# RWKV's two halves with buffers of their own, GDN behind them, gates as fp32 products

## The chip, the cores and the metric

The kernel runs on one core of a Trainium2 chip: five compute engines with a queue each (PE for matrix products, DVE for vector work, ACT for activations and copies, POOL for general vector work, SP, which here issues transfers) and 16 DMA engines, around an on-chip buffer (SBUF) and a small accumulator memory that PE writes (PSUM). The metric is the device time of one execution in microseconds, as the median of several runs. Each engine takes its instructions in the order in which the program has them and waits at each until its inputs and buffers are ready.

## The reference

The program is two networks, one behind the other, for 256 tokens of width 1024. The first (two feed-forward layers and four attention branches) isn't touched. The second is a mixing sublayer and a mixture of experts; the mixing sublayer takes the normed and modulated u and does this:

```python
a_lat, b_lat, gates_lat = jnp.split(u_lat @ w_in, split_at, axis=-1)
oa_lat, _ = run_a(a_lat, state_a)                      # gated DeltaNet (GDN)
ob_lat, _ = run_b(to_col_major(b_lat, rows), state_b)  # RWKV-7
y = jax.nn.sigmoid(g_a) * (o_a @ w_o_a) + jax.nn.sigmoid(g_b) * (o_b @ w_o_b)
return y @ w_out
```

Both branches are linear recurrences over the tokens, run in both directions. The step of RWKV is S = S(diag(w) + a bᵀ) + v kᵀ, y = S r; that of GDN is S = a(I - b k kᵀ)S + b k vᵀ, o = Sᵀ q. The states at the start come from a context sequence, which is done much earlier in the program. The output must be right to single precision.

## The kernel before

The recurrences are computed in chunks: for every chunk the products among its tokens form a triangular matrix, the inverse of which is found once for all chunks, and then a short chain carries the state from chunk to chunk. RWKV works on chunks of 64 tokens, four steps for each direction, and its eight heads go in two halves of four (`rwkv_half`, hf 0 and 1). A half has four parts:

- the *factors*: `first` makes decays, keys and their products from the projected columns (DVE lines 1520 to 1553: kdr, th, the scan cum, gam, AR, BK), `second` masks the products of tokens with tokens (Mak, Ur, Mr, lines 1569 to 1574), and copies bring the values into SV (line 1485);
- the *inverse* (`inverse`, lines 951 to 1046): a transposed copy Ut of the matrix, fifteen columns on DVE (pairs of Pb and Yb, lines 975 and 977), two transposes Yc, then small products on PE (ps_inv) with copies by DVE, ACT and POOL in between, to the last copy Ur. GDN's matrix is of 128 and takes one level more (D, Q, U, lines 1032 to 1045);
- the *gate* (`rwkv_gate`: pgate, yg, yz);
- the *chain* of four steps: rhs (line 1632), the product psa, its copy to SV (1638), the new state Sr (1657).

GDN (`gdn`, lines 1157 to 1345) has a setup (G, tv, row products rowp), normalised keys and queries, factors and products (Eb, E, U, qk), the same inverse, and a state chain (pks, r, Sa, oa).

In `mix` the projections come first: pieces of w_in are loaded, each is split into a rounded half wh (on ACT) and a rest wl (on DVE), and a product is three products of such halves (`mm3`, lines 102 to 104). Then RWKV is written with a high priority, then GDN and the gates. `gates_ahead` computes the 2048 gate columns: for 64 pieces of weights of 128x256 a load, the split wh on ACT (line 2229), wl on POOL (line 2230), and two `mm3`; it reads u back from DRAM, where the norm stored it in its two halves. Nothing before the merge needs its result, and the scheduler spreads its products over the stage. `merge` multiplies oa and ob with their output weights, applies the gates and makes the split of the merged product for the last projection; the experts follow, whose 96 MB of weights are streamed.

A scheduler decides the order of each engine's queue when the program is built, from the dependences, the buffers, priorities and its own estimate of durations. Buffers of a pool are handed out by tag; a tile of the same tag waits until the older one is no longer read. Both halves' sets (AR, BKT, U, R1, SV, Mr) had the same tags in one pool, so the second half's had to wait until the first half was through with them. In PSUM, RWKV had the tags g and s with two buffers each, and GDN with the gates had a (three buffers) and w (one).

Of the kernel before, what the change touches and what calls it, by code (L numbers as in the profile page):

```python
# [31 lines left out]
class Core:  # L32
# [142 lines left out]
    def norm_pair(self, pool, x, rs, A, B=None, keep=None, save=None):  # L175
# [7 lines left out]
        for t in range(2):  # L183
# [17 lines left out]
            if save is not None:  # L201
                for i, v in enumerate((hh, hl)):
                    nc.sync.dma_start(out=save[:, i, :, ts], in_=v[:, :, ts].bitcast(F32))
# [719 lines left out]
class Block2:  # L923
# [135 lines left out]
    def proj(self, u, w, start, n, evict):  # L1059
# [5 lines left out]
        for f0 in range(0, n, 256):  # L1065
            pg = k.ps("g", [P, 2, T], "pg")
            for g0 in range(f0, min(f0 + 256, n), wide):
                m = min(wide, n - g0)
                wr = k.raw(w[:, start + g0: start + g0 + m].rearrange("(c p) f -> p c f", p=P), [P, KC, m])
                for h0 in range(0, m, P):  # L1070
                    mm = min(P, m - h0)
                    fi = (g0 + h0 - f0) // P
                    for c0 in range(0, KC, cs):
# [286 lines left out]
class Rwkv(Block2):  # L1360
# [69 lines left out]
    def rwkv_proj(self, u, w, colmajor):  # L1430

        return tuple(self.rwkv_part(name, u, w, colmajor) for name in "vkwr")

    def rwkv(self, cols, S0, with_out, name, Sout=None, ob=None):


# [7 lines left out]

# [19 lines left out]
        out = None  # L1464
        for hf in range(2):

            SV = pool.tile([P, 2, 4, 4, 64], F32, tag="SV", name="SV")
            for d in range(2):
                vh = vT[:, 2 * hf:2 * hf + 2]
                if d == 1:  # L1470
                    vr = pool.tile([P, 2, T], F32, tag="t2", name="vTb", bufs=self.t2)
                    nc.vector.tensor_copy(vr, rev(vh))
                    vh = vr
                for t in range(2):
                    pt = k.ps("s", [P, 2, P], "ptv")
                    for p in range(2):
                        nc.tensor.transpose(pt[:, p], vh[:, p, t * P:(t + 1) * P], k.ident)
                    for q in range(2):
                        for h in range(2):
                            i = pt[64 * q:64 * q + 64, :, 64 * h:64 * h + 64]  # L1480
                            o = SV[64:128, h, 2 * t + q, 2 * d:2 * d + 2]
                            if h == 0:
                                nc.scalar.activation(o, i, AF.Copy)
                            else:
                                nc.vector.tensor_copy(o, i)
            out = self.rwkv_half(hf, kT, rT, lo, kk, SV, None if S0 is None else S0[:, hf],
                           with_out, name + str(hf), None if Sout is None else Sout[:, hf], vT, ob, out)
        if with_out:
            out()

    def rwkv_half(self, hf, kT, rT, lo, kk, SV, S0, with_out, name, Sout, vT, ob, before):
# [6 lines left out]
        R1 = pool.tile([P, 4, 4, 64], F32, tag="R1", name="R1")  # L1498
        gam = pool.tile([P, 4, 4], F32, tag="gam", name="gam")
        Mr = None  # L1500
        if with_out:
            Mr = pool.tile([P, 4, 2, 4, 64], F32, tag="Mr", name="Mr")
            bon = pool.tile([P, 2, 4], F32, tag="bon", name="bon")
# [101 lines left out]
        if before is not None:  # L1605
            before()
        XT = self.inverse(U, 16, 64)
        if with_out:
            gate = self.rwkv_gate(hf, bon, vT, lo[:, 2])
        if with_out:  # L1610
            yp = [k.ps("g", [P, 2, 2, 64], "yr") for _ in range(2)]

        def outputs(c, lhs, rhs, first, last):

            for d in range(2):
                cn = 3 - c if d else c
                for pl in range(2):
                    for h in range(2):
                        nc.tensor.matmul(yp[h][64 * (cn % 2):64 * (cn % 2) + 64, cn // 2, pl], lhs(h, 2 * d + pl),
                                         rhs(h, 2 * d + pl), start=first and pl == 0, stop=last and pl == 1)  # L1620

        hb = (slice(0, 64), slice(64, P))
        S = S0
        for c in range(4):
            rhs = R1[:, c]
            if S is not None:
                pa = k.ps("s", [P, 4, 64], "pa")
                for pd in range(4):
                    for b in (slice(0, 64), slice(64, P)):
                        nc.tensor.matmul(pa[b, pd], AR[b, pd, c, 0], S[b, pd], start=True, stop=True)  # L1630
                rhs = pool.tile([P, 4, 64], F32, tag="rhs", name="rhs")
                nc.vector.tensor_tensor(rhs, pa, R1[:, c], op=OP.add)
            px = [k.ps("s" if with_out else "g", [P, 4, 64], "psa") for _ in range(2)]
            for pd in range(4):
                for h, b in enumerate(hb):
                    nc.tensor.matmul(px[h][0:64, pd], XT[b, 4 * pd + c], rhs[b, pd], start=True, stop=True)
            nc.scalar.activation(SV[0:64, 0, c], px[0][0:64], AF.Copy)
            nc.vector.tensor_copy(SV[0:64, 1, c], px[1][0:64])
            if with_out:
                outputs(c, lambda h, pd: AR[hb[h], pd, c, 1], lambda h, pd: S[hb[h], pd], c == 0, False)  # L1640
            if c == 3 and with_out:
                outputs(c, lambda h, pd: Mr[:, pd, h, c], lambda h, pd: SV[:, h, c, pd], False, True)
                break
            pS = k.ps("s", [P, 4, 64], "pSr")
            for pd in range(4):
                for h in range(2):
                    b = slice(64 * h, 64 * h + 64)
                    nc.tensor.matmul(pS[b, pd], BKT[:, pd, c, b], SV[:, h, c, pd], start=True, stop=True)
            if c == 3:
                Sn = Sout  # L1650
            else:
                Sn = pool.tile([P, 4, 64], F32, tag="Sr", name="Sr", bufs=3)
            gb = gam[:, c].unsqueeze(2).to_broadcast([P, 4, 64])
            if S is None:
                nc.vector.tensor_tensor(Sn, pS, gb, op=OP.mult)
            else:
                nc.vector.tensor_tensor(Sn, pS, S, op=OP.add)
                (nc.vector if with_out else nc.gpsimd).tensor_tensor(Sn, Sn, gb, op=OP.mult)
            if with_out:
                outputs(c, lambda h, pd: Mr[:, pd, h, c], lambda h, pd: SV[:, h, c, pd], False, False)  # L1660
            S = Sn
        if not with_out:
            return
        y = self.keep.tile([P, 2, 256], F32, tag="yrw", name="yrw")
        for h in range(2):
            nc.scalar.activation(y.rearrange("p t (a h b) -> p h t a b", h=2, b=64)[:, h], yp[h], AF.Copy)
        return lambda: self.rwkv_out(hf, y, gate, ob)


class Tail(Rwkv):  # L1670
# [439 lines left out]
    def ctx_second(self):  # L2110

        k = self.k
        with k.use(g=k.banks["s"]):
# [3 lines left out]
            with k.pool("rcl", "right") as self.keep, k.pool("rc", "right") as self.pool:  # L2117
                self.t2 = 6
                self.rwkv(self.ctx_load("vkw") + [None], None, False, "rc", Sout=self.Sb)
# [27 lines left out]
    def begin(self, x, pool):  # L2147
# [4 lines left out]
        self.u_lat = self.dram.tile([P, 2, KC, T], F32, name="u_lat")  # L2152
        half = lambda v, q: v[:, q * 512:q * 512 + 512]
        with k.pool("lx", "right") as xp:
# [24 lines left out]
            with k.use(s=k.banks["a"]):  # L2179
                return k.norm_pair(xp, x, both, am, bm, pool, self.u_lat)  # L2180

    def mix(self, start):
# [4 lines left out]
        with ExitStack() as right, ExitStack() as left:  # L2187
            gk = self.gk = right.enter_context(k.pool("gk", "right"))
            gf = right.enter_context(k.pool("gf", "right"))
            proj = ExitStack()  # L2190
            up = proj.enter_context(k.pool("up", "right"))
            wp = Weights(proj.enter_context(k.pool("uw", "right")), 2048, 2, 1024, 3)
# [238 lines left out]
```

## Time and profile before

| | |
|---|---|
| median of 3 runs | 2396.19 us (2391.33 to 2402.87) |
| the profiled execution | 2390.7 us, of which the span 2389.0 |
| PE busy | 2249.9 us (94% of the span), mean granted clock 0.953 |
| DVE busy | 1689.7 us (71%) |
| ACT busy | 1199.8 us (50%) |
| POOL busy | 344.1 us (14%) |
| DMA | 450.91 MB, mean 189 GB/s |

The shares are means over stages that differ. The stage in question is short, from about 1633 to 2041 us of the span. The view by stage gives the busy time of each engine in a stretch and the clock that PE was granted; the view in order of time gives the start and length of each instruction, the number of equal ones merged into a row after the x, and, in brackets, how long the engine stood idle before it and what ended that.

### The profile page before, as it was taken

What the parts mean: (1) busy time and instruction counts of PE and PEld (TensorE: products, weight loads), DVE (VectorE), ACT (ScalarE), POOL (GpSimd) and SP (SyncE); (2) the same over time, 40 slices, a digit from 0 to 9 for tenths busy, and PEclk for the clock granted to TensorE, in tenths of its full rate; (3) what the DMA queues carried; (4) which work ended last, traced back from release to release, by engine and by line L of the source; (5) the groups of instructions that cost most, each with busy time, mean ns of one, the idle gap of its engine ahead of it and who ended that gap; (6) DMA issues with size and microseconds to landing.
All of it is one profiled execution on the core that took longest, in us unless ns stands there. A gap on an engine that the chain in (4) does not pass through costs nothing. (4 is left out here: it accounts for less than half of the span.)

```text
span 2389.0 us, 46279 instructions
## 1 busy us (share of the span) xinstructions
PE 2249.9 (94%) x19065; PEld 2041.7 (85%) x19065; DVE 1689.7 (71%) x2796; ACT 1199.8 (50%) x1919; POOL 344.1 (14%) x465
## 2 busy tenths in 40 slices
PE   7999999999999999999999999998989887899997
PEld 6999988897889888888888979998877777799996
DVE  6775575766665674675856668886885866789997
ACT  5554455555443543544554554443553313477775
POOL 2000112121200100100122210002245511000000
PEclk9999999999999989999999999998988668899999
DMA  9676344455434334342545468986445415699992
GB/s 327 223 248 202 111 150 143 140 166 188 142 125 163 132 112 152 128 142 68 173 130 166 143 211 299 331 285 185 125 133 161 146 40 193 239 374 351 353 352 98
DMA packets 325166, 450.91 MB, mean 189 GB/s; under 512 B 16122, under 2 KB 253236, under 8 KB 324564
## 3 DMA queue, kind: packets, MB, share of 16 engines
q1 hardware_dynamic: 324276, 447.06, 55.9%
q8 instruction: 152, 2.49, 0.4%
q0 software_dynamic: 672, 0.82, 0.3%
q14 instruction: 66, 0.54, 0.1%
HBM read 438.09 MB, written 9.76 MB: 187 GB/s over the span
## 5 line engine op out<-in xcount | busy, mean ns | idle before, releaser
L133 DVE TENSOR_TENSOR wl<-raw,wh 128x1024 fp32r<-128x1024 f32 (+1 forms) x703 | 860.0, 1230 | 364.4 <-ACT wh L132 355.2
L132 ACT ACTIVATE wh<-raw 128x1024 fp32r<-128x1024 f32 (+1 forms) x703 | 730.5, 1043 | 465.8 <-PE pg L104 189.5
L102 PE MATMUL pg<-hh,wl 128*128 128x256 f32 x2176 | 627.9, 289 | 4.9 <-DVE wl L133 4.4
L103 PE MATMUL pg<-hl,wh 128*128 128x256 f32 x2176 | 625.9, 288 | 0.4 <-DVE hl L133 0.4
L104 PE MATMUL pg<-hh,wh 128*128 128x256 f32 x2176 | 625.8, 288 | 0.0
L102 PEld LDWEIGHTS pg<-hh,wl 128*128 128x128 f32 x2176 | 420.1, 193 | 17.2 <-issue 6.0
L103 PEld LDWEIGHTS pg<-hl,wh 128*128 128x128 f32 x2176 | 420.0, 193 | 11.1 <-issue 6.6
L104 PEld LDWEIGHTS pg<-hh,wh 128*128 128x128 f32 x2176 | 420.1, 193 | 7.8 <-issue 6.4
L102 PE MATMUL ph<-wh,m0t 128*128 128x256 f32 x512 | 146.4, 286 | 0.0
L102 PE MATMUL acc<-wh,ul 128*128 128x512 f32 x352 | 137.9, 401 | 8.7 <-DVE ul L133 7.0
L103 PE MATMUL ph<-wl,m0t 128*128 128x256 f32 x512 | 144.2, 282 | 0.1
L104 PE MATMUL ph<-wh,m0t 128*128 128x256 f32 x512 | 143.7, 281 | 0.0
L104 PE MATMUL acc<-wh,uh 128*128 128x512 f32 x352 | 140.7, 400 | 0.0
L103 PE MATMUL acc<-wl,uh 128*128 128x512 f32 x352 | 140.4, 399 | 0.0
L103 PE MATMUL acc<-wl,hh 128*128 128x512 f32 (+2 forms) x320 | 120.5, 377 | 0.0
L104 PE MATMUL acc<-wh,hh 128*128 128x512 f32 (+2 forms) x320 | 120.4, 378 | 0.0
L102 PE MATMUL acc<-wh,hl 128*128 128x512 f32 (+2 forms) x320 | 116.9, 381 | 0.5 <-DVE hl L133 0.5
L103 PEld LDWEIGHTS ph<-wl,m0t 128*128 128x128 f32 x512 | 96.5, 189 | 1.2 <-DVE wl L133 0.4
L104 PEld LDWEIGHTS ph<-wh,m0t 128*128 128x128 f32 x512 | 96.5, 188 | 0.5
L102 PEld LDWEIGHTS ph<-wh,m0t 128*128 128x128 f32 x512 | 96.7, 189 | 0.1
L454 ACT ACTIVATE sg<-pg 128x256 f32<-128x256 f32 x80 | 30.8, 385 | 127.4 <-PE pg L104 123.8
L1705 DVE SCALAR_TENSOR_TENSOR adacc<-raw,silu_c,adacc 128x512 f32<-128x512 f32 x112 | 83.4, 747 | 15.3 <-DMA raw<-in_ada_w_dram 14.7
(712 smaller groups left out, 4214.5 us busy)
## 6 DMA issues: line engine op xcount, KB each, us to landing
raw<-in_ffn_w_gu_dram SPq DMA_DIRECT2D x88, 1024.0 KB
raw<-in_w_in_dram SPq DMA_DIRECT2D x56, 1024.0 KB
raw<-in_ffn_w_down_dram SPq DMA_DIRECT2D x44, 1024.0 KB
raw<-in_w_gate_dram SPq DMA_DIRECT2D x32, 1024.0 KB
raw<-in_moe_w_gate_dram SPq DMA_DIRECT2D x32, 1024.0 KB
raw<-in_moe_w_up_dram SPq DMA_DIRECT2D x32, 1024.0 KB
raw<-in_moe_w_down_dram SPq DMA_DIRECT2D x32, 1024.0 KB
raw<-in_ada_w_dram SPq DMA_DIRECT2D x48, 512.0 KB
```

The lines of the kernel that those rows point to most:

```text
L102: t.matmul(out, lhs[1], rhs[0], start=start, stop=False)
L103: t.matmul(out, lhs[0], rhs[1], start=False, stop=False)
L104: return t.matmul(out, lhs[0], rhs[0], start=False, stop=stop)
L132: return (nc.scalar.activation(h, src, AF.Copy), nc.vector.tensor_tensor(l, src, h.bitcast(F32), op=OP.subtract))
L133: nc.vector.tensor_tensor(l, src, h.bitcast(F32), op=OP.subtract))
L454: nc.scalar.activation(sg, pg[:, 0], AF.Silu)
L1705: nc.vector.scalar_tensor_tensor(acc, wv, sc, acc, op0=OP.mult, op1=OP.add)
```

## The change

The factors and the rest of `rwkv_half` are parted: the call does the factors and returns a closure `solve`, which does the inverse, the gate, the chain and the output. Half 0 has its sets in a pool ra, half 1 in a pool rb that is opened when the projections' pools are closed; the factors' temporaries lie in a pool fs. Half 1's factors use PSUM tag a, as GDN does. The priorities are 200000 for the first solve and 100000 for the factors and the second. RWKV's four projections are traced as w, k, r, v instead of v, k, w, r, GDN's before its z, and the projections' split weights have two buffers instead of three. `gates_ahead` is traced behind GDN and multiplies the raw weights with u in fp32, without split; u is added up from its halves by POOL in the norm and stays in SBUF (uf), so that neither the store nor the reloads of u are there. A load brings two pieces of weights.

```diff
     def rwkv_proj(self, u, w, colmajor):
-        return tuple(self.rwkv_part(name, u, w, colmajor) for name in "vkwr")
+        t = {name: self.rwkv_part(name, u, w, colmajor) for name in "wkrv"}
+        return tuple(t[name] for name in "vkwr")
...
+    def rwkv_half(self, hf, cols, kk, S0, with_out, name, Sout, ob, sets):
...
-        AR = pool.tile([P, 4, 4, na, 64], F32, tag="AR", name="AR")
-        BKT = pool.tile([P, 4, nb, P], F32, tag="BKT", name="BKT")
-        U = pool.tile([P, 16, 64], F32, tag="U", name="Ur")
+        AR = sets.tile([P, 4, 4, na, 64], F32, tag="AR", name="AR")
+        BKT = sets.tile([P, 4, nb, P], F32, tag="BKT", name="BKT")
+        U = sets.tile([P, 16, 64], F32, tag="U", name="Ur")
...
         second(*last)
-        if before is not None:
-            before()
-        XT = self.inverse(U, 16, 64)
...
+        def solve():
+            pool = self.pool
+            XT = self.inverse(U, 16, 64)
...
+            self.rwkv_out(hf, y, gate, ob)
+        return solve
...
-            wp = Weights(proj.enter_context(k.pool("uw", "right")), 2048, 2, 1024, 3)
+            wp = Weights(proj.enter_context(k.pool("uw", "right")), 2048, 2, 1024, 2)
...
+            ra, fs = ExitStack(), ExitStack()
+            seta = ra.enter_context(k.pool("ra"))
+            fsp = fs.enter_context(k.pool("fs"))
+            half = lambda hf, pool: self.rwkv_half(hf, cols, kk, self.Sb, True, "rl%d" % hf, None, ob, pool)
             with k.use(W=wp):
-                self.keep, self.pool, self.t2 = rk, rp, 4
+                self.keep, self.pool, self.t2 = rk, fsp, 4
                 cols = self.rwkv_proj(u, w, True)
                 with k.tc.high_priority(100000):
-                    self.rwkv(cols, self.Sb, True, "rl", None, ob)
+                    kk = self.rwkv_keys(cols, True)
+                    solve = [half(0, seta)]
                 with k.use(**G), k.pool("gp", "right") as self.pool:
                     self.keep, self.t2 = gk, 2
+                    gcols = self.gdn_proj(u, w, True)
                     self.gdn_z(u, w, oa)
-                    gcols = self.gdn_proj(u, w, True)
             proj.close()
-            with k.pool("gm", "right") as self.pool, k.use(W=Weights(gf, 256, 4, 256, 2), **G):
+            setb = right.enter_context(k.pool("rb", "right"))
+            with k.tc.high_priority(100000), k.use(**G):
+                self.keep, self.pool, self.t2 = rk, fsp, 4
+                solve.append(half(1, setb))
+            fs.close()
+            self.pool, self.t2 = rp, 3
+            with k.tc.high_priority(200000):
+                solve[0]()
+            ra.close()
+            with k.tc.high_priority(100000):
+                solve[1]()
+            with k.pool("gm", "right") as self.pool, k.use(W=Weights(gf, 512, 4, 0, 0), **G):
                 self.t2 = 4
-                self.gates_ahead(gf, a["w_in_2"][0][:, 3984:6032])
                 self.gdn_out(self.gdn(gcols, self.Sa, True, "gl"), oa)
+                self.gates_ahead(a["w_in_2"][0][:, 3984:6032])
...
-                    u = pool.tile([P, 2, 2, T], F32, tag="u", name="u", bufs=2)
-                    nc.sync.dma_start(out=u, in_=self.u_lat[:, :, c:c + 2])
-                wr = k.raw(w[c * P:c * P + P, d * P:(d + 2) * P], [P, 256])
-                ws = [k.W.parts.tile([P, 256], F32R, tag=tg, name=tg, bufs=k.W.npart) for tg in ("wh", "wl")]
-                nc.scalar.activation(ws[0], wr, AF.Copy)
-                nc.gpsimd.tensor_tensor(ws[1], wr, ws[0].bitcast(F32), op=OP.subtract)
+                    wr = k.raw(w[c * P:(c + 2) * P, d * P:(d + 2) * P].rearrange("(c p) f -> p c f", p=P), [P, 2, 256])
                 for j in range(2):
-                    js = slice(j * P, j * P + P)
-                    k.mm3(pg[:, j], (ws[0][:, js], ws[1][:, js]), (u[:, 0, c % 2].bitcast(F32R), u[:, 1, c % 2].bitcast(F32R)),
-                          c == 0 and j == 0, c == KC - 1 and j == 1)
+                    nc.tensor.matmul(pg[:, j], wr[:, c % 2, j * P:j * P + P], self.uf[:, c],
+                                     start=c == 0 and j == 0, stop=c == KC - 1 and j == 1)
```

What this does to the queues is seen at three places. On DVE before, in the first columns of half 0's inverse (Pb, Yb; cvo are evictions of GDN's convolution, G and tv the first instructions of GDN's body):

```order
L1093 SCALAR_TENSOR_TENSOR cvo<-pad,rowcols,cvo 128x256 x2
L975 TENSOR_TENSOR Pb<-Ub,Yb 128x1
L1093 SCALAR_TENSOR_TENSOR cvo<-pad,rowcols,cvo 128x256 x2
L977 TENSOR_REDUCE Yb<-Pb 128x1
L1170 TENSOR_TENSOR G<-pab,dtb 128x8
L1234 COPY tv<-cvo 128x1024
L975 TENSOR_TENSOR Pb<-Ub,Yb 128x4
```

DVE now, behind half 0's chain (SV is its last copy, st belongs to `rwkv_out`):

```order
L1646 COPY SV<-psa 64x256
L1173 TENSOR_TENSOR G<-pab,dtb 128x8
L1237 COPY tv<-cvo 128x1024
L1803 TENSOR_REDUCE st<-yrw 128x8
L1173 TENSOR_TENSOR G<-pab,dtb 128x8
L1804 TENSOR_SCALAR st<-st 128x8
L1805 TENSOR_TENSOR yrw<-yrw,st 128x512
L1176 TENSOR_SCALAR Be<-Be 128x16
```

GDN's first instructions went from the start of half 0's inverse to behind the end of half 0's chain.

On DVE before, at the start of GDN's inverse (qk and Ut are GDN's, kdr to AR are half 1's factors):

```order
L963 STREAM_TRANSPOSE Ut<-U 32x512 x2
L1276 TENSOR_TENSOR qk<-E,pkq 128x256
L1277 TENSOR_TENSOR qk<-E,pkq 128x256
L963 STREAM_TRANSPOSE Ut<-U 32x512 x2
L1520 TENSOR_SCALAR kdr<-th,rwc 128x256
L966 TENSOR_SCALAR Ub<-Ut,halves 128x256
L1524 TENSOR_SCALAR th<-th 128x512
L967 SCALAR_TENSOR_TENSOR Ub<-Ut,halves,Ub 128x256
```

DVE now, at the start of half 0's inverse (Mr is half 0's last factor, Ut and Ub are its inverse; AR and SV belong to half 1's factors):

```order
L1581 TENSOR_TENSOR Mr<-pm,minc 128x256
L962 STREAM_TRANSPOSE Ut<-Ur 32x512 x4
L1551 TENSOR_SCALAR AR<-kk 128x4 x4
L1499 COPY SV<-ptv 64x128 x2
L965 TENSOR_SCALAR Ub<-Ut,halves 128x256
L1499 COPY SV<-ptv 64x128 x2
L966 SCALAR_TENSOR_TENSOR Ub<-Ut,halves,Ub 128x256
L1499 COPY SV<-ptv 64x128 x2
```

Half 1's factors went from GDN's inverse to half 0's; GDN's inverse now stands behind half 1's chain.

On PE before, at GDN's setup (pg are gate products, rowp the row products that GDN's setup waits for):

```order
L104 MATMUL pg<-u,wh 128x256
L102 MATMUL pg<-u,wl 128x256
L103 MATMUL pg<-u,wh 128x256
L104 MATMUL pg<-u,wh 128x256
L1183 MATMUL rowp<-m_ge,G 4x128
L1184 MATMUL rowp<-ident,Be 4x128
L1183 MATMUL rowp<-m_ge,G 4x128
```

PE now, behind half 0's chain (psa and yr are its last step):

```order
L1627 MATMUL yr<-Sr,AR 64x64 x8
L1644 MATMUL psa<-rhs,Ur 64x64 x8
L1627 MATMUL yr<-SV,Mr 64x64 x8
L2252 MATMUL pg<-uf,raw 128x256 x15
L1186 MATMUL rowp<-m_ge,G 4x128
L1187 MATMUL rowp<-ident,Be 4x128
L1186 MATMUL rowp<-m_ge,G 4x128
```

The gate products are one pass each with raw weights; 15 of them stand between half 0's chain and GDN's row products, and 112 of the 128 lie between half 0's chain and GDN's inverse.

## Rows read from the trace of the kernel before

**Rows 1.** By stage: us, busy us (x) PE, PEld, DVE, ACT, POOL, PEclk, DMA, GB/s.
```profile
1757.00:1811.00 54.00, 40.26 (x733) 35.42 (x734) 35.48 (x86) 21.87 (x62) 24.84 (x33) 0.75 0.55 163
1811.00:1846.00 35.00, 32.66 (x432) 27.58 (x427) 19.43 (x45) 12.76 (x42) 19.68 (x22) 1.00 0.67 200
1846.00:1915.00 69.00, 59.26 (x388) 51.19 (x387) 56.07 (x126) 25.40 (x66) 37.72 (x47) 0.73 0.49 144
1915.00:1960.00 45.00, 35.05 (x1148) 32.21 (x1146) 28.48 (x69) 8.12 (x16) 5.54 (x13) 0.57 0.14 41
1960.00:1995.00 35.00, 32.05 (x451) 28.21 (x449) 21.74 (x51) 7.72 (x27) 1.67 (x1) 0.94 0.32 110
2083.00:2345.00 262.00, 260.83 (x1857) 243.50 (x1857) 238.74 (x248) 205.54 (x243) 0.00 (x0) 1.00 1.01 353
```

**Rows 2.** DVE in order of time, half 0: start, us, instruction [idle before <-releaser].
```profile
1758.22 4.34 DVE L963 STREAM_TRANSPOSE Ut<-Ur 32x512 f32<-32x512 f32 x4
...
1768.27 0.17 DVE L1170 TENSOR_TENSOR G<-pab,dtb 128x8 f32<-128x8 f32 x1
...
1806.02 0.68 DVE L1022 COPY Ur<-ps_inv 32x512 f32<-32x512 f32 x1
...
1811.41 0.42 DVE L1632 TENSOR_TENSOR rhs<-pa,R 128x256 f32<-128x256 f32 x1 [0.79 <-PE pa L1630]
...
1845.80 0.40 DVE L1638 COPY SV<-psa 64x256 f32<-64x256 f32 x1
```

**Rows 3.** DVE in order of time, half 1, GDN and merge.
```profile
1840.70 2.00 DVE L1544 TENSOR_SCALAR AR<-kk 128x4 f32<-128x4 f32 x4
...
1858.40 2.13 DVE L963 STREAM_TRANSPOSE Ut<-U 32x512 f32<-32x512 f32 x2
...
1914.88 2.12 DVE L963 STREAM_TRANSPOSE Ut<-Ur 32x512 f32<-32x512 f32 x2
...
1953.83 0.68 DVE L1045 COPY U<-ps_inv 64x512 f32<-64x512 f32 x1 [1.64 <-PE ps_inv L1044]
...
1957.69 0.68 DVE L1022 COPY Ur<-ps_inv 32x512 f32<-32x512 f32 x1 [0.63 <-PE ps_inv L996]
...
1994.34 0.75 DVE L1760 SCALAR_TENSOR_TENSOR oa<-pt,rowcols,oa 128x512 f32<-128x512 f32 x1 [0.72 <-PE pt L1758]
...
2011.68 1.23 DVE L133 TENSOR_TENSOR o<-ob,o 128x1024 fp32r<-128x1024 f32 x1 [2.56 <-ACT o L132]
...
2040.68 0.68 DVE L133 TENSOR_TENSOR u<-merged,u 128x512 fp32r<-128x512 f32 x1
```

**Rows 4.** Groups of DVE, half 0's inverse: xcount | busy, mean ns | idle before.
```profile
L1093 DVE SCALAR_TENSOR_TENSOR cvo<-pad,rowcols,cvo 128x256 f32<-128x256 f32 x11 | 5.0, 497 | 0.0
```

**Rows 5.** Groups of POOL, 1757 to 2000.
```profile
L2230 POOL TENSOR_TENSOR wl<-raw,wh 128x256 fp32r<-128x256 f32 x61 | 47.1, 776 | 61.1 <-ACT wh L2229 58.7 <-issue 2.1
```

**Rows 6.** Groups of DVE, half 1's factors: largest and smallest of eleven.
```profile
L1528 DVE TENSOR_TENSOR_SCAN cum<-reset,th 128x256 f32<-128x256 f32 x4 | 4.2, 1051 | 0.0
...
L1535 DVE COPY gam<-ee 128x4 f32<-128x4 f32 x4 | 1.2, 308 | 2.9 <-ACT ee L1533 2.9
```

**Rows 7.** DVE and POOL in order of time, 1868 to 1877.
```profile
1868.90 0.72 POOL L2230 TENSOR_TENSOR wl<-raw,wh 128x256 fp32r<-128x256 f32 x1 [0.60 <-ACT wh L2229]
...
1868.96 0.94 DVE L1552 TENSOR_TENSOR BK<-th,ee 128x256 f32<-128x256 f32 x1
...
1876.55 0.41 DVE L1552 TENSOR_TENSOR BK<-th,ee 128x256 f32<-128x256 f32 x1
```

**Rows 8.** PE in order of time, gate products and RWKV's gate.
```profile
1805.90 1.13 PE L1774 MATMUL pgate<-g,lo 128*128 128x256 f32 x4
...
1821.17 0.28 PE L102 MATMUL pg<-u,wl 128*128 128x256 f32 x1
...
1821.29 0.28 PE L103 MATMUL pg<-u,wh 128*128 128x256 f32 x1
...
1957.57 2.08 PE L1774 MATMUL pgate<-g,lo 128*128 128x256 f32 x4
```

More of the change, by code (lines that the diff above doesn't have):

```diff
@@ L173, in rms, with norm_pair @@
         return self.pow(pool, v, "%sr%d" % (name, t))
-    def norm_pair(self, pool, x, rs, A, B=None, keep=None, save=None):
+    def norm_pair(self, pool, x, rs, A, B=None, keep=None, full=None):
         nc = self.nc
@@ L200, in norm_pair @@
                 last = self.split(hh[:, js, ts], hl[:, js, ts], pt)
-            if save is not None:
-                for i, v in enumerate((hh, hl)):
-                    nc.sync.dma_start(out=save[:, i, :, ts], in_=v[:, :, ts].bitcast(F32))
+                if full is not None:
+                    nc.gpsimd.tensor_tensor(full[:, js, ts], hh[:, js, ts].bitcast(F32), hl[:, js, ts].bitcast(F32), op=OP.add)
             if t == 0:
@@ L1072, in proj @@
                     fi = (g0 + h0 - f0) // P
+                    if not isinstance(u, (tuple, list)):
+                        for c in range(KC):
+                            k.nc.tensor.matmul(pg[:mm, fi], wr[:, c, h0:h0 + mm], u[:, c], start=c == 0, stop=c == KC - 1)
+                        continue
                     for c0 in range(0, KC, cs):
@@ L1463, in rwkv @@
             nc.vector.tensor_tensor(kk[:, p], kk[:, p], pb, op=OP.mult)
-        out = None
+        return kk
+    def rwkv(self, cols, S0, name, Sout):
+        kk = self.rwkv_keys(cols, False)
         for hf in range(2):
[L1467 to L1487, printed above, removed]
@@ L1622, in rwkv_half @@
[L1622 to L1661, printed above, removed]
@@ L1662, in rwkv_half, with outputs @@
[L1662 to L1667, printed above, removed]
+        def solve():
+            pool = self.pool
+            XT = self.inverse(U, 16, 64)
+            if with_out:
+                gate = self.rwkv_gate(hf, bon, vT, lo[:, 2])
+            if with_out:
+                yp = [k.ps("g", [P, 2, 2, 64], "yr") for _ in range(2)]
+            def outputs(c, lhs, rhs, first, last):
+                for d in range(2):
+                    cn = 3 - c if d else c
+                    for pl in range(2):
+                        for h in range(2):
+                            nc.tensor.matmul(yp[h][64 * (cn % 2):64 * (cn % 2) + 64, cn // 2, pl], lhs(h, 2 * d + pl),
+                                             rhs(h, 2 * d + pl), start=first and pl == 0, stop=last and pl == 1)
+            hb = (slice(0, 64), slice(64, P))
+            S = S0
+            for c in range(4):
+                rhs = R1[:, c]
+                if S is not None:
+                    pa = k.ps("s", [P, 4, 64], "pa")
+                    for pd in range(4):
+                        for b in (slice(0, 64), slice(64, P)):
+                            nc.tensor.matmul(pa[b, pd], AR[b, pd, c, 0], S[b, pd], start=True, stop=True)
+                    rhs = pool.tile([P, 4, 64], F32, tag="rhs", name="rhs")
+                    nc.vector.tensor_tensor(rhs, pa, R1[:, c], op=OP.add)
+                px = [k.ps("s" if with_out else "g", [P, 4, 64], "psa") for _ in range(2)]
+                for pd in range(4):
+                    for h, b in enumerate(hb):
+                        nc.tensor.matmul(px[h][0:64, pd], XT[b, 4 * pd + c], rhs[b, pd], start=True, stop=True)
+                nc.scalar.activation(SV[0:64, 0, c], px[0][0:64], AF.Copy)
+                nc.vector.tensor_copy(SV[0:64, 1, c], px[1][0:64])
+                if with_out:
+                    outputs(c, lambda h, pd: AR[hb[h], pd, c, 1], lambda h, pd: S[hb[h], pd], c == 0, False)
+                if c == 3 and with_out:
+                    outputs(c, lambda h, pd: Mr[:, pd, h, c], lambda h, pd: SV[:, h, c, pd], False, True)
+                    break
+                pS = k.ps("s", [P, 4, 64], "pSr")
+                for pd in range(4):
+                    for h in range(2):
+                        b = slice(64 * h, 64 * h + 64)
+                        nc.tensor.matmul(pS[b, pd], BKT[:, pd, c, b], SV[:, h, c, pd], start=True, stop=True)
+                if c == 3:
+                    Sn = Sout
+                else:
+                    Sn = pool.tile([P, 4, 64], F32, tag="Sr", name="Sr", bufs=3)
+                gb = gam[:, c].unsqueeze(2).to_broadcast([P, 4, 64])
+                if S is None:
+                    nc.vector.tensor_tensor(Sn, pS, gb, op=OP.mult)
+                else:
+                    nc.vector.tensor_tensor(Sn, pS, S, op=OP.add)
+                    (nc.vector if with_out else nc.gpsimd).tensor_tensor(Sn, Sn, gb, op=OP.mult)
+                if with_out:
+                    outputs(c, lambda h, pd: Mr[:, pd, h, c], lambda h, pd: SV[:, h, c, pd], False, False)
+                S = Sn
+            if not with_out:
+                return
+            y = self.keep.tile([P, 2, 256], F32, tag="yrw", name="yrw")
+            for h in range(2):
+                nc.scalar.activation(y.rearrange("p t (a h b) -> p h t a b", h=2, b=64)[:, h], yp[h], AF.Copy)
+            self.rwkv_out(hf, y, gate, ob)
```

53 lines of the change are left out of this document (31 added, 22 removed).

## Prediction

> **What bounds the kernel now.** I read the busy time of the engines by stage first. The mix stage of the second block is the only part that the change reorders; I follow it from half 0's inverse at 1758 us to the last split of the merged product at 2041. Behind it the expert stage runs against memory: from 2083 to 2345 us the DMA share is 1.01 while PE is busy 260.83 of 262 us [rows 1], so nothing that arrives late there is won back later. In front of it, ffn2 is left as it was. What the change does to the time is therefore what it does to the moment at which the merge can begin.
>
> Inside the stage no engine is full: from 1757 to 1995 us DVE is busy 35.48 + 19.43 + 56.07 + 28.48 + 21.74 = 161 of 238 us, and PE's granted clock moves between 0.57 and 1.00 [rows 1]. It is a set of dependent chains. The second view, DVE's order of time, gives their ends. Half 0 of RWKV: the inverse starts at 1758.22 and ends with the copy of Ur at 1806.02, the first chain step is at 1811.41 and the last state values are copied at 1845.80 [rows 2]. Half 1: factors from 1840.70, and right behind the last of them its own inverse, from 1914.88 to 1957.69 [rows 3]. GDN: its inverse starts at 1858.40 and is done at 1953.83, and its output oa is there at 1994.34 + 0.75 = 1995.1 [rows 3]. So half 1's factors and inverse (117 us) lie beside GDN's inverse (95 us), and the two branches finish close together: oa at 1995.1, the split of ob at 2011.68, the last split of the merged product at 2040.68 [rows 3].
>
> **What the change moves.** The 74 us of half 1's factors are to stand beside half 0's inverse. The order of the changed program says that they do, and at what price: on DVE the first instruction of GDN's body stands behind the last chain step of half 0, where before it stood in the first columns of half 0's inverse, at 1768.27 us [rows 2]. Before, GDN had DVE's gaps from there on; now it begins when half 0 has ended. GDN's inverse and its state chain then have no RWKV work beside them at all, and they are last. So I add up one new chain: half 0's inverse (with half 1's factors), half 0's chain, half 1's inverse (with GDN's setup), half 1's chain (with GDN's factors), GDN's inverse alone, GDN's state chain alone, merge.
>
> 1. *Start of half 0's inverse.* 11 convolution evictions (5.0 us) that ran inside the inverse [rows 4] come ahead of it now. The load buffers of the projections fall from three pieces to two, for which no row gives a price: between 0 and 10 us. The gate subtraction on POOL that stood in the norm goes (1 to 3 us won). 16 gate products instead of 8 stand there, some 5 us of PE. I take 1758.2 + 5 = 1763, between 1757 and 1773.
>
> 2. *Half 0's inverse to its first chain step:* 53.2 us before [rows 2]. DVE was busy 35.48 of 54 us there [rows 1]. Out go the 5.0 us of evictions and about 8 us of GDN's setup; in come half 1's factors. Eleven groups of their instructions sum to 28.8 us of DVE, from the scan (4.2) to the copy of gam (1.2) [rows 6], and AR's scaling (2.0) and the eight SV copies add about 4 [rows 3]. POOL's subtraction costs DVE time while it runs: the product BK took 0.94 us when it started 0.06 us behind a subtraction, 0.41 without one [rows 7]. With the subtractions gone I take 5 off the 33. DVE: 35.5 - 5 - 8 + 28 = 50.5 us. Of the 18.5 us that it was idle for PE's inverse products I keep 7, since the factors fill the rest: 57.5, between 51 (no wait left) and 64. The first step comes at 1820.5.
>
> 3. *Half 0's chain:* 34.4 us before, with PE busy 32.66 of 35 us in gate products and GDN's [rows 1, 2]. Both are gone from there. The steps alone are between 18 and 25 us; I take 22: last copy at 1842.5, against 1845.8. So half 0 ends where it did, with half 1's factors done. That is the gain: half 1's inverse starts at about 1847 instead of 1914.9.
>
> 4. *Half 1's inverse to its first step.* It now has the neighbour that half 0's had, GDN's setup, so I take that length, 48.5 + 4.7 = 53 us (the evictions are gone from it, and 48 gate products stand in it instead). First step at 1900. Bounds 48 and 61.
>
> 5. *Half 1's chain with GDN's keys, factors and products, up to the start of GDN's inverse.* Before, the same work stood beside half 0's chain and ran from 1811.41 to 1858.40, 47.0 us [rows 2, 3], with some 8 us of half 1's copies in it, which go. On PE a gate product was three products at a spacing of 0.12 us, 0.36 us together [rows 8]; the fp32 product of the same shape is bounded by the gate's own fp32 pair, 1.13 us for two at full clock and 2.08 at the lower one [rows 8], so about 0.5 or 1.0 each. 64 of them stand here instead of 42 of the old, 32 us instead of 15. PE was nearly full there already, so part of it shows: 46 us, between 38 and 58. GDN's inverse starts at 1946.
>
> 6. *GDN's inverse alone.* Before, it took 95 us woven into half 1's work. Alone it is half 0's 48.5 us without the evictions (5.0), plus one more level of products and copies for blocks of 128, for which I allow 6: 50 us, between 44 and 58. End at 1996.
>
> 7. *GDN's state chain and output:* 1953.83 to 1995.1 before, 41 us, DVE busy 21.74 of 35 us of it with half 1's chain in the gaps [rows 1, 3]. Alone between 32 and 42, taken as 37: oa at 2033.
>
> 8. *Merge.* ob is long ready, so what remains behind oa is its split and products and what follows: from the split of ob at 2011.68 to the last split of the merged product at 2040.68 is 29.0 us [rows 3], with 4 for oa's way to its split, 33. It ends at 2066, against 2041.4 with that last split's own 0.68 us.
>
> The sum is 2066 - 2041.4 = 25 us later. The rest of the program keeps its length: the expert loads start when the stage's buffers are free and then need all of the DMA. The profiled execution took 2390.7 us (span 2389.0), so 2390.7 + 25 = **2415 us**; the median of the three runs lies 5.5 above that execution, inside their own spread. The removed reloads of u, gate splits on ACT and subtractions on POOL are free otherwise: none of those engines or queues is full between 1757 and 1995 (DMA share 0.14 to 0.67) [rows 1].
>
> **Rivals.** *(a) The subtractions were the drag.* 61 of them, 47.1 us, ran on POOL from 1757 to 2000 [rows 5]. If each had cost DVE the 0.53 us that BK lost [rows 7] and all of it lay on the chain, 32 us go and I have counted 5: 2415 - 27 = 2388. With half of that, 2401. Against it: DVE is idle a third of that time, and a longer instruction costs nothing where DVE waits for PE anyway. [...]
>
> *(b) The overlap pays after all.* If every stretch runs near its low end (51, 18, 48, 38, 44, 32, merge 31, started at 1758), the merge ends at about 2026: 15 us earlier, 2376. The mechanism would be PE's clock in GDN's inverse and state chain: from 1915 to 1960 the same kinds of products ran at a clock of 0.57 with PE busy 35.05 of 45 us [rows 1], and an inverse alone with a full clock would get half of that back. It decides if GDN's inverse takes under 40 us, or half 1's chain with GDN's factors under 35.
>
> *(c) The fp32 gates hold up PE's queue.* 112 gate products stand between half 0's last step and GDN's inverse. At the lower clock, 1.0 each [rows 8], they take 112 us where steps 4 and 5 have 99, and the rest of PE's work there waits in the same queue: 30 us more, 2445. It decides if the granted clock is under 0.7 there.
>
> *(d) Half 1's factors don't run beside half 0's inverse.* The order of the program excludes it; a wait for memory could not, but the new buffers have none.
>
> **How the numbers follow.** About 0.5% (12 us) is what a measurement of this kernel tells from no change: faster is under 2384, slower over 2408. The forecast, 2408 to 2432, has 0.45, (c) 0.12, (a) in the band of no change 0.20, (b) or (a) in full 0.23. So faster 0.23, same 0.20, slower 0.57. The range leaves out the lower half of the faster cases and the end of (c): 2378 to 2445; the forecast's own range is 2400 to 2432.
>
> **What would show it.** Right: in the changed trace half 1's last Mr stands before half 0's first chain step or just behind it, half 1's Ut at about 1847, GDN's Ut at about 1946, oa at about 2033 and 77 us after half 1 could have finished. Step 2 is wrong if half 0's first step comes before 1812 or behind 1830; step 5 if PE is idle over a quarter of it; steps 6 and 7 if GDN's inverse and chain together take under 75 us. The whole is wrong if GDN's inverse starts before 1920: with 87 us for steps 6 and 7 oa is then where it was, and the earlier ob is won.

## The result, and the profile after

The changed kernel takes 2415.89 us (median of six runs, 2413.26 to 2421.47), the kernel before 2397.72 in the six runs beside them: a ratio of 1.0079 with a 95% interval of 1.0065 to 1.0093, slower by 0.8%. The forecast was 2415. The profiled execution has a span of 2413.9 us, 24.9 more than before; by the medians the change costs 18.2 us.

By stage (us, busy us and instructions of PE, PEld, DVE, ACT, POOL, then PEclk, DMA share and GB/s), cut at the new chain's own borders, to be read beside [rows 1]:

```profile
1766.00:1825.00 59.00, 37.35 (x704) 31.64 (x703) 46.09 (x114) 17.29 (x42) 14.82 (x21) 0.56 0.04 8
1825.00:1846.00 21.00, 17.37 (x301) 15.42 (x299) 8.24 (x21) 2.66 (x7) 0.00 (x0) 0.77 0.01 2
1849.00:1897.00 48.00, 40.00 (x664) 32.97 (x663) 25.38 (x70) 11.95 (x36) 10.24 (x11) 0.82 0.34 94
1897.00:1946.00 49.00, 48.88 (x485) 38.98 (x483) 25.95 (x57) 9.47 (x29) 14.29 (x13) 1.00 0.29 83
1946.00:1992.00 46.00, 29.41 (x687) 26.53 (x688) 27.06 (x67) 6.21 (x13) 3.93 (x6) 0.63 0.10 31
1992.00:2027.00 35.00, 25.47 (x149) 23.18 (x148) 16.00 (x38) 7.24 (x24) 3.03 (x5) 0.70 0.34 121
```

And DVE in order of time (start, length, instruction, in brackets the idle time before it and what ended it), beside [rows 2, 3]:

```profile
1766.48 4.21 DVE L962 STREAM_TRANSPOSE Ut<-Ur 32x512 f32<-32x512 f32 x4
...
1825.10 0.42 DVE L1640 TENSOR_TENSOR rhs<-pa,R 128x256 f32<-128x256 f32 x1 [0.17 <-PE pa L1638]
...
1845.76 0.42 DVE L1646 COPY SV<-psa 64x256 f32<-64x256 f32 x1 [0.81 <-PE psa L1644]
1846.10 0.15 DVE L1173 TENSOR_TENSOR G<-pab,dtb 128x8 f32<-128x8 f32 x1
...
1846.92 0.69 DVE L1237 COPY tv<-cvo 128x1024 f32<-128x1024 f32 x1 [0.67 <-PE yr L1627]
...
1849.13 4.19 DVE L962 STREAM_TRANSPOSE Ut<-Ur 32x512 f32<-32x512 f32 x4
...
1903.15 0.42 DVE L1640 TENSOR_TENSOR rhs<-pa,R 128x256 f32<-128x256 f32 x1 [1.86 <-PE pa L1638]
...
1945.47 4.25 DVE L962 STREAM_TRANSPOSE Ut<-U 32x512 f32<-32x512 f32 x4
...
1955.32 0.41 DVE L1646 COPY SV<-psa 64x256 f32<-64x256 f32 x1
...
1990.99 0.68 DVE L1044 COPY U<-ps_inv 64x512 f32<-64x512 f32 x1 [1.02 <-PE ps_inv L1043]
...
2025.68 1.41 DVE L1769 SCALAR_TENSOR_TENSOR oa<-pt,rowcols,oa 128x512 f32<-128x512 f32 x2 [1.00 <-PE pt L1767]
...
2062.03 0.68 DVE L133 TENSOR_TENSOR u<-merged,u 128x512 fp32r<-128x512 f32 x1
```

Half 0's chain ends at 1845.8, to a tenth of a microsecond where it ended before, and half 1's factors are done by then: half 1's inverse starts 66 us earlier than in [rows 3]. But GDN's first instruction G stands right behind half 0's last copy, where before it stood at 1768, and its inverse starts at 1945 instead of 1858. With little of RWKV left beside it (half 1's fourth step, whose last copy SV is at 1955.32, and its output), GDN's inverse and state chain take 81.6 us in a row, and oa comes 32 us later than before. The merge, for which ob now waits, gives 11 of these back: its last split is 21.4 us later. Another 3.5 us lie behind it.

### The profile page after: what moved, and what is told of

Same layout as the page of the kernel before. It is cut to its first block, busy times and chain, and to the rows that moved or that the text cites. A ratio compares the mean times of both kernels' runs of the same rounds, so it can differ in the third digit from the quotient of the medians.

```text
span 2413.9 us, 45647 instructions
## 1 busy us (share of the span) xinstructions
PE 2260.4 (94%) x18937; PEld 2042.9 (85%) x18937; DVE 1678.1 (70%) x2796; ACT 1178.9 (49%) x1858; POOL 298.1 (12%) x405
```

## The experiments

Two theories. M: GDN stands late because of memory. GDN's pool is now laid over half 0's sets and the factors' temporaries, where before it lay over what the projections had left; a tile there waits until half 0 has read its own for the last time. G, the rival (not the tile G of the rows): the plain fp32 gate products fill PE between half 0's chain and GDN's inverse (48.88 of 49 us busy from 1897 to 1946), and they are the loss.

The memory part of M can be read without a run. In the program as built, GDN's pool takes bytes 98496 to 159616 of each partition of SBUF, half 0's set 82368 to 121376; before, GDN's pool lay at 137504 to 198624, all of it memory that the projections had left. And in the rows above tv, a copy of cvo, waits by the profile for PE's yr, which it doesn't read: yr reads half 0's Mr, over part of which tv lies. What that place costs is what the runs have to show.

**GDN's early tiles elsewhere.** GDN's tiles are given to four pools instead of one, so that those of its setup lie over the projections' memory and most of its keys' and factors' over that of the factors' temporaries; only bv and U lie over half 0's set. Its factors also get buffers that they no longer share with its inverse:

```diff
-        G = pool.tile([P, 2, 2, 4], F32, tag="G", name="G")
+        G = first.tile([P, 2, 2, 4], F32, tag="G", name="G")
...
-        kd = pool.tile([P, 4, 4, P], F32, tag="kd", name="kd")
+        kd = mid.tile([P, 4, 4, P], F32, tag="kd", name="kd")
...
-        U = pool.tile([P, 4, 4, P], F32, tag="U", name="U")
+        U = low.tile([P, 4, 4, P], F32, tag="U", name="U")
...
-            with k.pool("gm", "right") as self.pool, k.use(W=Weights(gf, 512, 4, 0, 0), **G):
+            with k.pool("ge", "right") as self.first, k.pool("gh", "right") as self.mid, k.pool("gl", "left") as self.low, k.pool("gm", "right") as self.pool, k.use(W=Weights(gf, 512, 4, 0, 0), **G):
```

> The changed kernel, with GDN's tiles placed otherwise: its setup, keys and factors lie over the projections' and the factors' freed buffers instead of over half 0's sets (only bv and U lie there now). Theory M (GDN is last because its first tiles wait for half 0's sets to be read for the last time): GDN's first instruction moves from behind half 0's fourth step to behind its first, GDN's inverse starts at about 1925 instead of 1945, oa comes about 20 us earlier, 2396 us (2388 to 2404). Theory G (the fp32 gates fill PE and that is what the 24 us are): GDN's setup gains nothing, 2408 or more.

Measured: 2386.94 us, 0.9957 of before (0.9941 to 0.9974) and 29 us less than the changed kernel, with no instruction taken away. DVE in order of time:

```profile
1822.61 0.42 DVE L1643 TENSOR_TENSOR rhs<-pa,R 128x256 f32<-128x256 f32 x1 [1.30 <-PE pa L1641]
...
1832.49 0.17 DVE L1176 TENSOR_TENSOR G<-pab,dtb 128x8 f32<-128x8 f32 x1
...
1858.42 0.69 DVE L1123 COPY qtok<-ptk 128x512 f32<-128x512 f32 x1 [1.27 <-ACT qtok L1121]
...
1859.10 4.21 DVE L963 STREAM_TRANSPOSE Ut<-Ur 32x512 f32<-32x512 f32 x4
...
1910.56 0.41 DVE L1643 TENSOR_TENSOR rhs<-pa,R 128x256 f32<-128x256 f32 x1
...
1913.27 2.13 DVE L963 STREAM_TRANSPOSE Ut<-U 32x512 f32<-32x512 f32 x2
...
1970.07 0.68 DVE L1045 COPY U<-ps_inv 64x512 f32<-64x512 f32 x1 [0.52 <-PE ps_inv L1044]
...
2000.06 0.74 DVE L1773 SCALAR_TENSOR_TENSOR oa<-pt,rowcols,oa 128x512 f32<-128x512 f32 x1
```

G moved up by 14 us only, into half 0's chain, but GDN's setup and its keys and queries (qtok) are then nearly done when half 1's inverse begins, and GDN's inverse starts 32 us earlier and runs beside half 1's chain. M's direction holds; the gain is larger than expected (29 us for 20, below the range of 2388 to 2404), and GDN's inverse starts at 1913 where 1925 was expected. This version is faster than both kernels, if by 0.4% only against the one before.

**One gate product in eight.** The rest of the products is left out of the changed kernel:

```diff
                 for j in range(2):
-                    nc.tensor.matmul(pg[:, j], wr[:, c % 2, j * P:j * P + P], self.uf[:, c],
-                                     start=c == 0 and j == 0, stop=c == KC - 1 and j == 1)
+                    if c == 0:
+                        nc.tensor.matmul(pg[:, j], wr[:, c % 2, j * P:j * P + P], self.uf[:, c],
+                                         start=j == 0, stop=j == 1)
```

> The changed kernel with one of eight gate products computed (the other seven eighths of the gate product are left out; their weights are still loaded). Theory M: PE's 112 gate products behind half 0's chain are partly cover, partly in the way; rhs of half 1 to GDN's inverse shrinks from 42 us to about 33, in all 8 to 16 us less, 2400 to 2408. Theory G: the gates are the whole of the loss, 2392 or less.

Measured: 2393.18 us, 22.7 less than the changed kernel. That is beyond what M expected and just short of G. By stage, half 1's inverse and half 1's chain up to GDN's inverse, first in the changed kernel and then here:

```profile
1849.00:1903.00 54.00, 46.00 (x721) 38.09 (x721) 29.60 (x76) 13.79 (x45) 10.24 (x11) 0.84 0.32 90
1903.00:1945.00 42.00, 41.88 (x401) 32.93 (x395) 20.76 (x49) 7.63 (x20) 14.16 (x12) 1.00 0.31 89
...
1849.00:1902.00 53.00, 34.24 (x646) 26.61 (x646) 32.95 (x79) 19.62 (x59) 14.33 (x14) 0.61 0.47 142
1902.00:1924.00 22.00, 21.98 (x280) 16.93 (x279) 19.02 (x45) 4.62 (x9) 10.61 (x9) 1.00 0.01 1
```

Half 1's inverse is as long with the 13 gate products that are left there as with the changed kernel's 54 (53 us for 54); the chain, which had 41 of them and now has none, lost 20 of its 42. At 0.45 us a product (16 records, two to a product, in 3.62 us at a granted clock of 1.00 in the changed kernel) 41 are 18.5 us, and PE was busy nearly all of that stretch in both. So gate products do cost time beside this chain. Whether that tells the two kernels apart depends on what they cost in the old order.

**The fp32 gates alone.** The kernel before with the new `gates_ahead`, uf and loads, and nothing else of the change.

> The kernel before with the fp32 gates alone (plain products of the raw weights with u, which POOL adds up; no split, no reload of u), its gates at the place and priority that they had. Theory M: within 4 us of before, 2394 to 2402. Theory G: slower by 15 or more, 2412.

Measured: 2394.98 us, 0.9988 (0.9973 to 1.0004), no difference clear of noise, as M expected. G's short form, that plain fp32 products are the loss, falls for the old order.

**One gate product in eight, old order.** First with the old gates, which keep their splits and subtractions:

> The kernel before with one of eight gate products computed (the rest of the gate product is left out; loads, splits and subtractions stay). If the old order hides the gates beside its two overlapped branches, and their exposure is a part of what the change lost: 2386 to 2396 (2 to 12 us gained). If the gates cost as much in the old order as in the new one (22.7 us there): 2375, and the gates are no part of the difference.

Measured: 2416.34 us, slower than before, where both expectations had it faster. This run can't be read: with the products gone the scheduler put what was left elsewhere. Half 0's inverse already starts 13.6 us later than before (1771.8 for 1758.2), and PE, in half 0's first step, sat in front of a gate product whose subtraction was not there yet (PE in order of time):

```profile
1840.90 0.58 PE L102 MATMUL pg<-u,wl 128*128 128x256 f32 x1 [10.82 <-POOL wl L2230]
```

Then with the fp32 gates, which have no subtraction to wait for:

> The kernel of e3 (old order, fp32 gates) with one of eight gate products computed (the rest of the gate product is left out, the loads stay); unlike e6 it has no subtractions whose order can hold PE. If the old order hides its gate products: within 8 us of e3, 2387 to 2397. If they cost as much there as in the changed order (22.7 us): 2372.

Measured: 2372.27 us, 22.7 less than e3. The gate products cost 22.7 us in the old order and 22.7 in the changed one; that the two agree to a tenth is chance, as each of the four medians has runs several us to either side, and the scheduler laid each program out anew. But they are no part of the difference that these runs could tell, so the last form of G falls, and with e9 beside it e2 doesn't speak for G.

**The old gates in the changed kernel.**

```diff
-                self.gates_ahead(a["w_in_2"][0][:, 3984:6032])
+                self.gates_ahead(gf, a["w_in_2"][0][:, 3984:6032])
...
+                nc.scalar.activation(ws[0], wr, AF.Copy)
+                nc.gpsimd.tensor_tensor(ws[1], wr, ws[0].bitcast(F32), op=OP.subtract)
```

> The changed kernel with the old gates (split on ACT and POOL, three fp32r products, u reloaded), everything else as changed. Theory M: 64 products beside half 1's chain take 0.36 us instead of 0.45 on PE, 6 us less, the subtractions give DVE some of it back: 2408 to 2418. Rival (the kind of the gate products is what costs): 2400 or less.

Measured: 2424.96 us, 9.1 more than the changed kernel. Both theories missed: in the new order the fp32 gates, with all that they spare, are worth 9 us. So they are a gain there and not the loss. Half 1's chain up to GDN's inverse took 35 us (1908 to 1943) for 42, 7 less where the expectation had 6, but GDN's inverse, beside which gates now stood, took from 1943 to 2001, 58 us for 46, with POOL busy 22.39 us there against 3.93:

```profile
1828.00:1853.00 25.00, 22.65 (x305) 20.17 (x302) 8.01 (x21) 2.43 (x7) 0.00 (x0) 0.50 0.01 1
...
1943.00:2001.00 58.00, 43.78 (x779) 39.88 (x778) 31.45 (x65) 16.54 (x38) 22.39 (x32) 0.74 0.60 176
```

DVE's waits for the inverse's products on PE are 24.4 us in that stretch against 17.1 in the changed kernel's. Whether POOL or PE's own gate products made them, this run doesn't part. Nor is that the whole of it: half 1's inverse already starts 7.7 us later (1856.8 for 1849.1), 4 of them from half 0's chain, which took 25 us for 21 at a granted clock of 0.50 for 0.77 (first row above) with no gate product in it; half 1's inverse and chain together win 10 back.

**Gates at another place.** In the changed kernel the gates are traced behind the projections and load into memory that these leave:

```diff
             proj.close()
+            gq = right.enter_context(k.pool("gq", "right"))
+            with k.use(W=Weights(gq, 512, 4, 0, 0), **G):
+                self.gates_ahead(gq, a["w_in_2"][0][:, 3984:6032])
```

> The changed kernel with the gates traced right behind the projections, their loads in memory that the projections leave: half of the products then stand beside half 0's inverse and the other half beside its chain, none behind GDN's row products. Theory M: half 0's end 5 to 10 us later (PE's queue), half 1's inverse and chain 15 to 20 shorter, so 2403 to 2412. Theory G: the gates cost the same wherever they stand, 2412 to 2420.

Measured: 2416.02 us, as the changed kernel. That is what G's expectation said, that the gates cost the same wherever they stand; M's 2403 to 2412 was missed. By stage, half 0's inverse, its chain with GDN's start, and half 1's chain up to GDN's inverse:

```profile
1765.00:1825.00 60.00, 51.59 (x773) 41.51 (x772) 45.07 (x112) 17.15 (x41) 15.74 (x21) 0.86 0.28 79
1825.00:1873.00 48.00, 47.80 (x476) 39.33 (x476) 11.07 (x29) 8.24 (x21) 0.00 (x0) 1.00 0.43 125
1925.00:1945.00 20.00, 20.00 (x225) 15.47 (x227) 16.53 (x40) 3.17 (x6) 10.51 (x10) 0.91 0.01 2
```

Half 1's chain became 23 us shorter and half 0's longer by as much. The 48 products beside half 0's inverse added 14 us of PE's busy time and 2 us to its length (60.4 for 58.6).

**Gates beside the inverses alone.** Memory as in e1; 48 products behind the projections, 48 queued on PE behind half 0's last step, 32 behind GDN's products:

```diff
+            with k.use(W=Weights(gq, 512, 4, 0, 0), **G):
+                self.gates_ahead(gq, a["w_in_2"][0][:, 3984:6032], (6, 8, 10), (self.pe_ins,))
```

> The kernel of e1_gdn_early with its gates in three places: 48 products traced behind the projections (their loads in memory that the projections leave), 48 queued on PE behind half 0's last step, 32 behind GDN's products. e4 had its 48 products beside half 0's inverse and lost 0.4 us there; e2 shows no gain beside half 1's inverse. Theory (a gate product costs time only where a chain's steps wait in PE's queue, and nothing beside an inverse's columns): the 30 products fewer beside half 1's chain and GDN's inverse, 0.45 us each, give 13 us: 2374 (2368 to 2382). Rival (PE's queue costs the same wherever they stand): 2387 (2383 to 2391).

Measured: 2385.30 us, 0.9960 (0.9944 to 0.9975); e1 has 2386.94. The expected 13 us did not come; the rival (the same cost wherever they stand) had 2383 to 2391. DVE in order of time, to be read beside e1's:

```profile
1849.56 4.24 DVE L963 STREAM_TRANSPOSE Ut<-Ur 32x512 f32<-32x512 f32 x4
...
1893.93 0.41 DVE L1643 TENSOR_TENSOR rhs<-pa,R 128x256 f32<-128x256 f32 x1
...
1908.79 2.14 DVE L963 STREAM_TRANSPOSE Ut<-U 32x512 f32<-32x512 f32 x2
...
1955.34 0.68 DVE L1045 COPY U<-ps_inv 64x512 f32<-64x512 f32 x1 [1.02 <-PE ps_inv L1044]
...
1988.91 0.75 DVE L1773 SCALAR_TENSOR_TENSOR oa<-pt,rowcols,oa 128x512 f32<-128x512 f32 x1
```

In the profiles, from half 1's Ut to oa e1 takes 141.7 us and this kernel 140.1: half 1's inverse up to its first step is 7 shorter (44.4 for 51.5), GDN's inverse 10 (46.5 for 56.8), but 12 us lie between half 1's first step and GDN's inverse that were not there (14.9 for 2.7), and GDN's state chain is 4 longer at a clock of 0.75 (1956 to 1990) instead of 0.90 (1973 to 2002). The profiled execution of this kernel (2378.02 us) is the fastest of its ten, and its oa comes 11 us earlier than e1's, 9.5 of them won ahead of half 1's inverse; the medians differ by 1.6 us in all, so the profiles can't be taken for the typical run to a few us.

**GDN's setup freed of the shared PSUM buffers too.** The kernel of e1, with GDN's setup in PSUM tag w and traced ahead of half 1's factors:

```diff
+            with k.use(**dict(G, s=("w", 1))):
+                self.pool, self.t2 = rp, 4
+                gdn = self.gdn(gcols, self.Sa, True, "gl")
+                next(gdn)
             setb = right.enter_context(k.pool("rb", "right"))
```

> The kernel of e1_gdn_early with GDN's setup and its keys' transposes in PSUM tag w (one buffer, that of the gates) instead of a, and traced ahead of half 1's factors; GDN's first instruction then stands right behind the start of half 0's inverse, where the old order had it. If, with the memory free, the PSUM buffers shared with half 1's factors are the next thing that holds GDN: its inverse starts about 15 us earlier than in e1 (1898 instead of 1913), oa about 10 earlier, 2377 (2370 to 2384). If DVE or PE is by then full enough between half 0's inverse and GDN's: no gain, 2385 to 2390.

Measured: 2388.91 us, 0.9974 (0.9959 to 0.9989). G starts at 1763.5 instead of 1832.5 and GDN's inverse at 1896.6 instead of 1913.3, as expected, yet the inverse ends at 1960.8 instead of 1970.8 and oa at 1998.1 instead of 2000.8: beside GDN's inverse half 1's chain now starts later (first step at 1920.3 instead of 1910.6), and PE is busy 47.44 of 49 us from 1912 to 1961:

```profile
1763.49 0.16 DVE L1175 TENSOR_TENSOR G<-pab,dtb 128x8 f32<-128x8 f32 x1
...
1896.58 2.08 DVE L963 STREAM_TRANSPOSE Ut<-U 32x512 f32<-32x512 f32 x2
...
1920.29 0.42 DVE L1646 TENSOR_TENSOR rhs<-pa,R 128x256 f32<-128x256 f32 x1 [1.01 <-PE pa L1644]
...
1912.00:1961.00 49.00, 47.44 (x1013) 40.09 (x1012) 23.91 (x48) 8.41 (x18) 3.44 (x5) 0.96 0.24 70
```

That is the second expectation, no gain. So the PSUM buffers or the place in the program, which this run changes together, did hold GDN's start in e1, and an earlier start won nothing.

## Why the prediction was right, point by point

The forecast was made as a sum of eight stretches. Beside what the trace shows:

| step | forecast, us | measured, us |
|---|---|---|
| 1 start of half 0's inverse | 1763 | 1766.5 |
| 2 to its first chain step | 57.5 | 58.6 |
| 3 half 0's chain | 22 | 21.1 |
| half 1's inverse starts | 1847 | 1849.1 |
| 4 to its first chain step | 53 | 54.0 |
| 5 to GDN's inverse | 46 | 42.3 |
| 6 GDN's inverse alone | 50 | 46.2 |
| 7 state chain, oa | 37 | 35.4 |
| 8 merge | 33 | 35.6 |
| end of the merge | 2066 | 2062.7 |

Every stretch lies inside the bounds that it was given. That the sum hit to a microsecond is partly luck. Its 25 us were laid on the profiled execution of the kernel before, 2390.7 us, which was faster than all six timed runs of that kernel; by the medians the change is 18.2 us, and the same sum laid on the median of three, 2396.19, would have said 2421. Besides, the merge ended 3.3 us sooner than forecast, and the 3.5 us behind the merge, which the forecast held constant, made up for it; 3 of them lie in the expert stage and were not followed.

*The main step was right and is shown.* GDN behind half 0's chain was read from the order of the queue; e1 shows that this place is what costs, since moving GDN's tiles alone wins 29 us. The forecast did not say why GDN stood there. The reason is memory; the PSUM buffers shared with half 1's factors or the place in the program come next, and e8 shows that an earlier start won nothing more. "No RWKV work beside them at all" was a little too much: half 1's fourth step ran in the first 10 us of GDN's inverse.

*Step 2.* The size was right, its make-up less so: DVE was busy 46.09 us instead of 50.5, and waited 13 instead of 7. Of the 18.5 us that the forecast put down to PE's inverse products, 11.7 were waits for them; 6.1 of these are left now, close to the 7 kept. What the sum hadn't counted is 5.1 us in which half 1's factors wait for ACT (th, ee) in the middle of half 0's inverse.

*Step 5.* The sum was right to 4 us, its make-up not: 41 gate products ran in this stretch and not 64, and nearly all of their time shows and not a part of it (20 of the 42 us in e2).

*Rival (a), the subtractions,* did not come in: the time is 2416 and not 2388 or 2401. No run takes the subtractions alone; with the splits, the reloads and the other products that go with them, e7 has 9 us in this order and e3 nothing clear of noise in the old one. Of half 1's eight products BK before, three took 0.94 to 0.97 us and five 0.40 to 0.41; [rows 7] has one of each, and the forecast put the difference down to the subtraction. In e3, which has no gate subtraction, two of the eight took 1.50 and 1.48 us and six 0.39 to 0.42, so the pair doesn't show the subtraction as the cause, and the price of 27 us that rival (a) drew from it for the whole kernel no run shows. *Rival (b), everything at its low end:* none of its points of decision was reached, GDN's inverse took 46 us and not under 40. *Rival (c), the gates at the lower clock:* the clock was 0.82 and 1.00 in steps 4 and 5. A product, two records in the trace, took 0.45 us at a granted clock of 1.00 (16 records in 3.62 us), where most of them ran; only some of step 4's took longer (14 records in 6.12 us at 0.53, 12 in 4.00 us at 0.69). Its 30 us were not worked out either: 112 us of products beside stretches of 99 make 13. *Rival (d)* was excluded rightly. The last sign of being wrong was set loosely: with GDN's inverse at 1920 and 87 us behind it, oa would have come at 2007 and not where it was, at 1995.

*One thing missed.* The forecast counted 16 gate products among the projections and asked no more. These ran at 1640 to 1653, but their result stood on ACT behind half 0's whole chain (gth at 1847.2), the store of it (line 2256) on SP, and the loads of further gate weights behind that store. Ahead of it on SP, a load for RWKV's gate (line 1777) had waited about as long. The view puts the store's wait down to Be, which follows gth on ACT. Waits of the DMA queue of SP (line, waited for, us in total, times, longest):

```profile
SPq L1777 <- DVE kdr L1527: 54.1, 1, 54.1
SPq L2256 <- ACT Be L1175: 49.4, 1, 49.4
```

And PE's first gate product behind half 0 (in order of time):

```profile
1847.86 6.74 PE L2252 MATMUL pg<-uf,raw 128*128 128x256 f32 x30 [0.98 <-ACT gth L2255]
```

From 1766 to 1846 the DMA share was 0.04 and less, and no gate product ran. Weights for the next ones were there, as they ran from 1847.9 on and the next load was issued at 1849.9 only; what they waited for was gth, which reads the one PSUM buffer of the gates. So the gth of the first group, and not the loads alone, held the other 112 products behind half 0; why the scheduler set it so late was not followed. In e4 and e5 gate products do run there, and neither gained anything clear of noise by it.

## What to carry to other kernels

Two buffers that are made separate take memory from a third thing: look at what the freed and new pools now lie on, because a tile waits for the last reader of whatever had its place (here tv for yr), and the order of the queues shows it before any run. Here that place was worth 29 us. Work that becomes the last in a row is priced by its length alone (GDN's inverse and state chain here, 81.6 us), and the gain of the overlapped part counts only until that work starts. And filler on PE's queue cost about its own length where PE was busy all the time (half 1's chain, e2: 20 us for 41 products of 0.45 us) and next to nothing beside half 1's inverse (1 us for 41 products); but that is no rule for placing it: e4 moved it from one chain to the other and e5 put most of it beside inverses, and neither won anything clear of noise.

## What the runs showed of the hardware

Work taken from PE did not always give its time back. In e2 half 1's inverse kept 13 of its 54 gate products, and PE's granted clock in that stretch fell from 0.84 to 0.61; the stretch took 53 us instead of 54. In e4 half 0's inverse got 48 products, the clock rose from 0.56 to 0.86, and the stretch took 60 us instead of 59. In both the number of products and the clock moved together and the length stayed within 2 us. Whether the higher clock is what paid for the products stays open; no run held the clock and changed the products alone.
